# Starting layer 0's output projection with the context tiles inside the last attention block

## The chip, the cores and the metric

The kernel runs on one core of a Trainium2 chip. Five engines work from their own instruction queues and wait for each other through semaphores: TensorE (PE, with its weight loads PEld) for matrix products, VectorE (DVE), ScalarE (ACT), GpSimd (POOL), and SyncE (SP), whose queue issues nearly all DMA transfers here. The metric is the device time of one execution in microseconds (us). The kernel before takes 1860.38 us, the median of three runs between 1852.12 and 1868.84.

## The reference

Two layers over 1024 latent tokens and 256 context tokens of width 1024. Layer 0 is multi-head latent attention with 16 heads, layer 1 differential attention with 8 heads. The core of layer 0 is:

```
q, k, v, gate     = project(h, True)      # 1024 latent tokens, rotary
q_c, k_c, v_c, gate_c = project(h_c, False)   # 256 context tokens
o   = dense_attention(q, concat(k, k_c), concat(v, v_c), scale)
o_c = dense_attention(q_c, k_c, v_c, scale)
x   = layer_norm(ALPHA * x   + gate_x * ((o   * silu(gate))   @ out_w[0]), ln_g, ln_b)
ctx = layer_norm(ALPHA * ctx + gate_c * ((o_c * silu(gate_c)) @ out_w[0]), ln_g, ln_b)
```

The context tokens attend to context keys only, and both streams share the output weights `out_w[0]` and the layer norm.

## The kernel before

Tokens are cut in ten tiles of 128: tiles 0 to 7 are latent, 8 and 9 are context. To keep precision, a float32 matrix is split into a high part and a remainder (`split`, L175 to L177: ACT copies, DVE or POOL subtracts), and a product is the sum of three products (`mm3`, L184 to L187).

**Attention.** For each head h the queries are in three blocks: 0 and 1 are 512 latent tokens each, 2 is the 256 context tokens. `units0` cuts a block into units of two key tiles: five units for blocks 0 and 1, one for block 2. A unit computes scores on PE (L770 to L772), exp and a half-precision copy on ACT (L714, L715), the remainder on POOL (L716), and then 24 products with V on PE (L782 to L785, twelve per key tile). `run_step` writes PE's order by hand: the products with V lag two units behind the scores (`LAG`, `pend`, `retire`), and side work (the maxima of the next block, the projections of the next head) is put between by counts per unit. At a block's end DVE divides by the sum (L793, L794), and after every second head SP stores the pair of heads to `o_d[0]` in DRAM (L798). In the last head the order is blocks 0, 2, 1, with a store for each block.

**Who orders what.** PE's order is the written one inside `run_step`. The orders of ACT, DVE, POOL and SP come from a scheduler that ranks the program's instructions. So work that is written in the last head can be placed earlier, if its data and buffers are ready. `load_outw` (L803 to L808) loads the eight 512 KB slices of `out_w[0]` and splits them on ACT (L807) and DVE (L808); it is written in the last head and needs the space of the projection weights.

**Output of layer 0.** After the last head the attention's buffers and banks are closed. Then `out_tile` runs for tiles 8, 9, 0, ..., 7: load o from `o_d` and the stored silu(gate) g from `sg_d` (L858, L859), multiply on POOL (L860), transpose eight 128x128 blocks on PE (L866), split, multiply by the output weights (24 products for each half of 512 columns, into one bank each), then on DVE gate, residual and statistics (L877 to L879), a power on POOL (L159, L160), and the normalisation (L883). Behind it z is transposed back (L918), scaled and shifted into `hb` (L920 on DVE, L922 on POOL) and split into layer 1's input (L925, L926). For latent tiles the residual of layer 1 is prepared too (L911 to L913). The scaled ln_g and ln_b that this needs are loaded ahead of tile 0 (L905, L906); ln_g takes the buffer `gate01`, which held the context tokens' gate.

```
for t in (8, 9, 0, 1, 2, 3, 4, 5, 6, 7):
    if t == 0:
        for j, (src, tag) in enumerate(((ln_g, "gate01"), (ln_b, "gb1"))):
            gb.append(op0.tile([P, D], F32, tag=tag, bufs=1, name=nm("gb")))
            bcast_row(gb[j], src[0:1, :])
            pool.tensor_scalar(gb[j], gb[j], ALPHA, None, op0=ALU.mult)
    s = 0 if t < 8 else 1
    z = out_tile(t, oH, oL, gate[s], res0, op0)
```

Of the kernel before, what the change touches and what calls it, by code (L numbers as in the profile page):

```python
# [9 lines left out]
F32 = mybir.dt.float32  # L10
# [7 lines left out]
P = 128  # L18
D = 1024
# [34 lines left out]
def hybrid_kernel(  # L54
# [473 lines left out]
    with spool("p0g") as pg:  # L528
# [14 lines left out]
        for _ in side:  # L543
# [23 lines left out]
    cosA = wk.tile([P, SEQ], F32, name="cosA")  # L567
    sinA = wk.tile([P, SEQ], F32, name="sinA")
# [5 lines left out]
    def w0(tag, dt=None):  # L574
        sh, d, b = TAG0[tag]
        return rot(wk, sh, d, tag, b)

    wv = [w0("p32").bitcast(F32R) for _ in range(2)]
    wvs = w0("p32")
    for hh in range(2):  # L580
# [241 lines left out]
            pass  # L822
    man.close()
    ow_ctx = ExitStack()
    for h in range(H0):
        last = h == H0 - 1
        even, quad = (h + 1) % 2 == 0, (h + 1) % 4 == 0
        if last:
            rp.close()
            ow = ow_ctx.enter_context(spool("o0w", side="right"))  # L830
            oH = ow.tile([P, KT, D], F32R, name="oH0")
            oL = ow.tile([P, KT, D], F32R, name="oL0")
            run_step(units0(h, 0) + units0(h, 2), [(max0(h, 2), (1, 0, 1)), (max0(h, 1), (0, 1, 1, 1, 2, 1)),
                                                   (load_outw(oH, oL, lambda: w0("ows")), (1, 2, 2, 2, 1))])
            run_step(units0(h, 1), [])
        else:
            kq = chain(prod_k(h + 1), prod_q(h + 1, 0))
            run_step(units0(h, 0), [(max0(h, 1), (1, 1, 2, 1, 1)), (max0(h, 2), (0, 1, 0, 1)),
                                    (kq, (2, 2, 1 + quad, 0, 0) if even else (2,))])
            qs = chain(prod_q(h + 1, 1), prod_q(h + 1, 2))  # L840
            run_step(units0(h, 1) + units0(h, 2), [(max0(h + 1, 0), (1, 1, 1, 2, 1)),
                                                   (qs, (1, 1 + quad, 0, 1) if even else (2,))])
# [7 lines left out]
    def bcast_row(dst, src):  # L850
        sp.dma_start(dst, src.to_broadcast([P, D]))

    def out_tile(t, oH, oL, gate, res_fn, tp):
# [5 lines left out]
        sp.dma_start(g, sg_d[0][ts, :])  # L859
        pool.tensor_tensor(o, o, g, op=ALU.mult)  # L860
        tH = tp.tile([P, KT, P], F32R, tag="tH", bufs=2, name=nm("tH"))
        tL = tp.tile([P, KT, P], F32R, tag="tL", bufs=2, name=nm("tL"))
        for hh in range(2):
            tb = bank("c")
            for j in range(4):
                pe.transpose(tb[:, j * P:(j + 1) * P], o[:, (hh * 4 + j) * P:(hh * 4 + j + 1) * P], idn)  # L866
            hi = tH[:, hh * 4:hh * 4 + 4, :].rearrange("p a b -> p (a b)")
            split(hi, tL[:, hh * 4:hh * 4 + 4, :].rearrange("p a b -> p (a b)"), tb)
# [3 lines left out]
        for hh in range(2):  # L872
            c = slice(hh * 512, hh * 512 + 512)
            y = bank("ab"[hh])
            for k in range(KT):
                mm3(y, tH[:, k, :], tL[:, k, :], oH[:, k, c], oL[:, k, c], k == 0, k == KT - 1)
            dve.tensor_tensor(z[:, c], y, gate[:, c], op=ALU.mult)  # L877
            dve.scalar_tensor_tensor(z[:, c], res[:, c], rmul, z[:, c], op0=ALU.mult, op1=ALU.add)
            dve.bn_stats(bs[:, hh, :], z[:, c])  # L879
# [3 lines left out]
        dve.tensor_scalar(z, z, mv[:, 0:1], mv[:, 2:3], op0=ALU.subtract, op1=ALU.mult)  # L883
        return z

    with ow_ctx, spool("o0") as op0:
        gate = [op0.tile([P, D], F32, tag=f"gate0{s}", bufs=1, name=f"gate0{s}") for s in range(2)]
        for s in range(2):
            bcast_row(gate[s], gates_d[0, s:s + 1, :])
        gb = []  # L890

        zres = {}

        def res0(t):
            r = op0.tile([P, D], F32, tag="res", bufs=2, name=nm("res"))
            src = xr[t * P:(t + 1) * P, :] if t < 8 else ctxr[(t - 8) * P:(t - 7) * P, :]
            sp.dma_start(r, src)
            zres[t] = r
            return r, ALPHA

        for t in (8, 9, 0, 1, 2, 3, 4, 5, 6, 7):
            if t == 0:
                for j, (src, tag) in enumerate(((ln_g, "gate01"), (ln_b, "gb1"))):
                    gb.append(op0.tile([P, D], F32, tag=tag, bufs=1, name=nm("gb")))
                    bcast_row(gb[j], src[0:1, :])  # L905
                    pool.tensor_scalar(gb[j], gb[j], ALPHA, None, op0=ALU.mult)  # L906
            s = 0 if t < 8 else 1
            z = out_tile(t, oH, oL, gate[s], res0, op0)
            if t < 8:
                zr = zres[t]  # L910
                dve.tensor_tensor(zr, z, gb[0], op=ALU.mult)  # L911
                pool.tensor_tensor(zr, zr, gb[1], op=ALU.add)
                sp.dma_start(zn_d[t * P:(t + 1) * P, :], zr)  # L913
            hb = op0.tile([P, KT, P], F32, tag="hb", bufs=1, name=nm("hb"))
            for hh in range(2):
                tb = bank("d")
                for j in range(4):
                    pe.transpose(tb[:, j * P:(j + 1) * P], z[:, (hh * 4 + j) * P:(hh * 4 + j + 1) * P], idn)  # L918
                ks = slice(hh * 4, hh * 4 + 4)
                dve.tensor_tensor(hb[:, ks, :], tb.rearrange("p (a b) -> p a b", a=4),  # L920
                                  ab1[:, 0, ks, s:s + 1].to_broadcast([P, 4, P]), op=ALU.mult)
                pool.tensor_tensor(hb[:, ks, :], hb[:, ks, :],  # L922
                                   ab1[:, 1, ks, s:s + 1].to_broadcast([P, 4, P]), op=ALU.add)
# [558 lines left out]
```

## Time and profile before

| | us |
|---|---|
| median of three runs | 1860.38 |
| the runs | 1852.12, 1868.84, 1860.38 |
| span of the profiled execution | 1870.0 |
| last product of the attention starts | 804.95 |
| first transposes of output tile 8 / tile 9 / tile 0 | 818.10 / 832.78 / 846.61 |
| last z transposes of the output stage | 973.72 |

The profiled execution is one more execution than the three runs; its span, from the first to the last instruction, is the time that its trace gives. In the rows of a timeline the first number is the start in us from the span's beginning, the second the length. Then come engine, line, operation, output and inputs with their shapes, and in brackets how long the engine stood idle before and what released it. In a group row "x8" is the number of instructions; three numbers with slashes are the shortest, median and longest duration in ns. Names are those of the program without buffer numbers: ps_a to ps_d are PSUM banks, p/ph/pl the exponentials and their two half-precision parts, tH/tL the transposed and split o·g, z the normalised output. PEclk is the share of full speed that TensorE's clock was granted.

### The profile page before, as it was taken

How to read it: one execution, taken by the hardware profiler on the slowest of the kernel's cores; microseconds unless marked ns; L12 is line 12 of the kernel's file. 1: busy time of each engine (PE TensorE's matmuls, PEld its weight loads, DVE VectorE, ACT ScalarE, POOL GpSimd, SP SyncE). 2: the span in 40 equal slices, each digit the busy share in tenths (PEclk: the TensorE clock that was granted, in tenths of full speed). 3: DMA queues.
4: the chain of work that ended last, by engine and by line, in shares of the span. 5: the costliest groups of instructions: out<-in, count | busy, mean ns of one | idle time of the engine just before them, and what ended most of it. 6: DMA issues, size and time to landing. Idle time of an engine off the chain costs nothing. (4 is left out here: it accounts for less than half of the span.)

```text
span 1870.0 us, 36547 instructions
## 1 busy us (share of the span) xinstructions
PE 1696.2 (91%) x14468; PEld 1237.0 (66%) x14468; DVE 1245.6 (67%) x2072; ACT 1077.1 (58%) x2143; POOL 835.2 (45%) x741
## 2 busy tenths in 40 slices
PE   7889998999999998868979999999999999988998
PEld 3888965656666565556756576767666666666776
DVE  7546766565565657526764777787877777878674
ACT  3432047867777787711123667676767676767542
POOL 1443026767767676646662213222222222433654
PEclk9999799999999999979999999999999999999999
DMA  8245630111111113043333222222121212224341
GB/s 307 62 126 182 189 108 18 39 33 36 42 44 32 32 41 100 25 164 123 124 127 106 71 63 66 62 64 58 56 49 44 59 46 61 63 53 139 99 131 68
DMA packets 111225, 154.84 MB, mean 83 GB/s; under 512 B 13415, under 2 KB 84679, under 8 KB 111054
## 3 DMA queue, kind: packets, MB, share of 16 engines
q1 hardware_dynamic: 104238, 146.22, 26.1%
q10 hardware_dynamic: 6816, 6.29, 1.0%
q8 instruction: 114, 1.87, 0.4%
q14 instruction: 57, 0.47, 0.1%
HBM read 98.65 MB, written 27.07 MB: 67 GB/s over the span
## 5 line engine op out<-in xcount | busy, mean ns | idle before, releaser
L716 POOL TENSOR_TENSOR pl<-p,ph 128x1024 f16<-128x1024 f32 (+1 forms) x176 | 362.8, 2066 | 155.9 <-ACT ph L715 129.5
L1167 ACT ACTIVATE p<-ps_b,mx 128x512 f32<-128x512 f32 (+1 forms) x384 | 230.6, 618 | 83.1 <-DVE mx L1163 82.7
L696 DVE TENSOR_REDUCE mx<-ps_a 128x1 f32<-128x1024 f32 x128 | 155.6, 1223 | 138.2 <-PE ps_a L694 138.2
L714 ACT ACTIVATE p<-ps_a,esc 128x1024 f32<-128x1024 f32 (+1 forms) x176 | 189.2, 1075 | 100.4 <-PE ps_a L772 94.5
L715 ACT CAST ph<-p 128x1024 f16<-128x1024 f32 (+1 forms) x176 | 177.1, 1006 | 5.5
L1161 DVE TENSOR_REDUCE mx<-ps_b 128x1 f32<-128x512 f32 x256 | 165.6, 682 | 0.0
L785 PE MATMUL ps_d<-Vh,pl 128*128 128x65 f16 x1344 | 147.5, 195 | 5.2 <-POOL pl L716 5.1
L782 PE MATMUL ps_d<-Vh,ph 128*128 128x65 f16 x1344 | 149.5, 196 | 0.0
L784 PE MATMUL ps_d<-Vl,ph 128*128 128x64 f16 x1344 | 148.3, 193 | 0.0
L185 PE MATMUL ps_b<-h1H,wH 128*128 128x512 f16 (+1 forms) x384 | 133.5, 348 | 14.1 <-DVE pl L182 6.7
L185 PE MATMUL ps_b<-wH,h1H 128*128 128x256 f16 x512 | 139.5, 272 | 4.4 <-ACT p L1167 4.2
L1192 POOL TENSOR_TENSOR sm<-sm,us 128x1 f32<-128x1 f32 x64 | 18.3, 285 | 271.9 <-DVE sm L1171 258.6
L187 PE MATMUL ps_b<-wH,h1L 128*128 128x256 f16 x512 | 139.5, 273 | 0.0
L186 PE MATMUL ps_b<-wL,h1H 128*128 128x256 f16 x512 | 139.5, 272 | 0.0
L1144 PE MATMUL ps_b<-KS,QS 128*128 128x512 f16 (+1 forms) x384 | 126.1, 345 | 12.0 <-DVE pl L182 6.1
L782 PEld LDWEIGHTS <-ph 128*128 128x128 f16 x1344 | 124.2, 98 | 18.4 <-issue 5.5
L187 PE MATMUL ps_b<-h1H,wL 128*128 128x512 f16 (+1 forms) x384 | 133.2, 347 | 0.8 <-DVE wL L182 0.8
L186 PE MATMUL ps_b<-h1L,wH 128*128 128x512 f16 (+1 forms) x384 | 133.4, 347 | 0.0
L784 PEld LDWEIGHTS <-ph 128*128 128x128 f16 x1344 | 124.9, 99 | 12.4 <-issue 0.8
L770 PE MATMUL ps_a<-qH,KH 100*128 100x512 f16 x320 | 123.6, 386 | 9.7 <-ACT p L714 4.3
L1145 PE MATMUL ps_b<-KS,Q 128*128 128x512 f16 (+1 forms) x384 | 129.1, 345 | 0.0
L785 PEld LDWEIGHTS <-pl 128*128 128x128 f16 x1344 | 124.1, 98 | 6.6 <-POOL pl L716 6.5
(370 smaller groups left out, 5161.9 us busy)
## 6 DMA issues: line engine op xcount, KB each, us to landing
ws<-in_dw SPq DMA_DIRECT2D x30, 512.0 KB, 3.8
adw<-in_ada_w SPq DMA_DIRECT2D x24, 512.0 KB, 5.0
g<-sg_d SPq DMA_DIRECT2D x18, 512.0 KB, 3.7
adaw<-in_ada_w SPq DMA_DIRECT2D x16, 512.0 KB, 7.1
sg_d<-gg ACTq DMA_DIRECT2D x40, 128.0 KB, 2.8
o<-o_d SPq DMA_DIRECT2D x10, 512.0 KB, 3.5
o_d<-op SPq DMA_DIRECT2D x7, 640.0 KB, 3.7
xt<-in_xT SPq DMA_DIRECT2D x16, 256.0 KB, 3.6
```

The lines of the kernel that those rows point to most:

```text
L185: pe.matmul(ps, aH, bH, start=start, stop=False, skip_group_check=skip)
L186: pe.matmul(ps, aH, bL, start=False, stop=False, skip_group_check=skip)
L187: pe.matmul(ps, aL, bH, start=False, stop=stop, skip_group_check=skip)
L696: dve.tensor_reduce(mx[:, t, 0:1], ps, axis=AX.X, op=ALU.max)
L714: act.activation(p32[:, :n], st, AF.Exp, scale=esc0)
L715: act.copy(ph[:, :n], p32[:, :n])
L716: pool.tensor_tensor(pl[:, :n], p32[:, :n], ph[:, :n], op=ALU.subtract)
L782: pe.matmul(pv[:, t, :], ph[:, ts], Vh[:, k, h, :], start=(k == kcs[0] and t == 0), stop=False, skip_group_check=True)
L784: pe.matmul(pv[:, t, :V0], ph[:, ts], Vl[:, k, h, :], start=False, stop=False, skip_group_check=True)
L785: pe.matmul(pv[:, t, :], pl[:, ts], Vh[:, k, h, :], start=False, stop=(k == NT - 1), skip_group_check=True)
L1161: dve.tensor_reduce(mx[:, 2 + 2 * m + i:3 + 2 * m + i], b, axis=AX.X, op=ALU.max, negate=True)
L1167: act.activation(p[m][:, c0:c0 + n], b, AF.Exp, bias=nb, accum_out=sm[:, 2 + 3 * m + i:3 + 3 * m + i])
```

## The change

Output tiles 8 and 9 begin inside the last head. `load_outw` is started in head 14 and its steps are spread over heads 14 and 15. The cosine and sine tables move to a rotating tag `cs` of two buffers, so that after the last rotary use these two, `rsw`, `rr` and the two `ows` are free and hold o, g and the transposed parts of both context tiles. During the last block o and g are loaded, DVE multiplies them, and PE takes the transposes and products of both tiles between and behind the last units. The results stay in two pairs of banks (`yctx`) until the output stage, whose `out_tile` is cut in `out_y` (up to the products) and `out_z` (from the gate on). Both context tiles' `out_z` is written ahead of the loop. The banks are set anew after that.

```diff
-            "ows": ([P, D], F32, 2)}
+            "ows": ([P, D], F32, 2), "cs": ([P, SEQ], F32, 2)}
...
+    def turn_out(o, hH_, hL_, tb, hh):
+
+        for j in range(4):
+            pe.transpose(tb[:, j * P:(j + 1) * P], o[:, (hh * 4 + j) * P:(hh * 4 + j + 1) * P], idn)
+        f = lambda x: x[:, hh * 4:hh * 4 + 4, :].rearrange("p a b -> p (a b)")
+        split(f(hH_), f(hL_), tb)
+
+    def mm_out(y, tH, tL, c):
+        for k in range(KT):
+            mm3(y, tH[:, k, :], tL[:, k, :], oH[:, k, c], oL[:, k, c], k == 0, k == KT - 1)
...
-        if last:
+        if h == H0 - 2:
             rp.close()
...
+            lw = load_outw(oH, oL, lambda: w0("ows"))
+        if last:
             run_step(units0(h, 0) + units0(h, 2), [(max0(h, 2), (1, 0, 1)), (max0(h, 1), (0, 1, 1, 1, 2, 1)),
-                                                   (load_outw(oH, oL, lambda: w0("ows")), (1, 2, 2, 2, 1))])
-            run_step(units0(h, 1), [])
+                                                   (lw, (1, 0, 1))])
+            octx = {t: (w0(b_), w0(a_))[::-1] for t, a_, b_ in ((8, "rsw", "rr"), (9, "cs", "cs"))}
+
+            def load_ctx():
+                yield
+                yield
+                for t in (8, 9):
+                    for x, d_ in zip(octx[t], (o_d[0], sg_d[0])):
+                        sp.dma_start(x, d_[t * P:(t + 1) * P, :])
+                    dve.tensor_tensor(*[octx[t][0]] * 2, octx[t][1], op=ALU.mult)
+                yield
+
+            run_step(units0(h, 1), [(load_ctx(), (1, 1, 1))])
+            tv = lambda x: x.bitcast(F32R).rearrange("p (a b) -> p a b", a=KT)
+            tctx = {8: (tv(w0("ows")), tv(w0("ows"))), 9: (tv(w0("rr")), tv(w0("cs")))}
+            with tc.manual_schedule(engines={ENG[c] for c in MAN}):
+                for t in (8, 9):
+                    tb = pair()
+                    for hh in range(2):
+                        turn_out(octx[t][0], *tctx[t], tb[:, hh * 512:hh * 512 + 512], hh)
+                    if t == 8:
+                        retire(0)
+                        retire(1)
+                for t in (8, 9):
+                    yctx[t] = pair()
+                    for hh in range(2):
+                        c = slice(hh * 512, hh * 512 + 512)
+                        mm_out(yctx[t][:, c], *tctx[t], c)
+                        flush()
...
-    flush()
     a0.close()
-    set_banks(a=2, b=2, c=2, d=2)
...
-        for s in range(2):
+        for s in (1, 0):
             bcast_row(gate[s], gates_d[0, s:s + 1, :])
...
+        zctx = {t: out_z([yctx[t][:, :512], yctx[t][:, 512:]], gate[1], res0, t, op0) for t in (8, 9)}
+        set_banks(a=2, b=2, c=2, d=2)
         for t in (8, 9, 0, 1, 2, 3, 4, 5, 6, 7):
...
-            z = out_tile(t, oH, oL, gate[s], res0, op0)
+            z = out_z(out_y(t, op0), gate[0], res0, t, op0) if t < 8 else zctx[t]
```

More of the change, by code (lines that the diff above doesn't have):

```diff
@@ L576, in w0 @@
         return rot(wk, sh, d, tag, b)
+    cosA, sinA = w0("cs"), w0("cs")
     wv = [w0("p32").bitcast(F32R) for _ in range(2)]
@@ L824, in hybrid_kernel, with first @@
     ow_ctx = ExitStack()
+    def first(g, n):
+        for _ in range(n):
+            next(g)
+            yield
[7 more added lines that the diff above has]
+            mm3(y, tH[:, k, :], tL[:, k, :], oH[:, k, c], oL[:, k, c], k == 0, k == KT - 1)
+    yctx = {}
     for h in range(H0):
@@ L836, in hybrid_kernel @@
         else:
             kq = chain(prod_k(h + 1), prod_q(h + 1, 0))
+            low = [[(first(lw, 3), p_)] if h == H0 - 2 else [] for p_ in ((1, 0, 1, 0, 1), (1, 0, 1, 0, 1))]
             run_step(units0(h, 0), [(max0(h, 1), (1, 1, 2, 1, 1)), (max0(h, 2), (0, 1, 0, 1)),
-                                    (kq, (2, 2, 1 + quad, 0, 0) if even else (2,))])
+                                    (kq, (2, 2, 1 + quad, 0, 0) if even else (2,))] + low[0])
             qs = chain(prod_q(h + 1, 1), prod_q(h + 1, 2))
@@ L851, in bcast_row, with out_y @@
         sp.dma_start(dst, src.to_broadcast([P, D]))
-    def out_tile(t, oH, oL, gate, res_fn, tp):
+    def out_y(t, tp):
         ts = slice(t * P, (t + 1) * P)
@@ L863, in out_tile, with out_z @@
         for hh in range(2):
[L864 to L868, printed above, removed]
+            turn_out(o, tH, tL, bank("c"), hh)
+        for hh in range(2):
+            y = bank("ab"[hh])
+            mm_out(y, tH, tL, slice(hh * 512, hh * 512 + 512))
+            yield y
+    def out_z(ys, gate, res_fn, t, tp):
         z = tp.tile([P, D], F32, tag="z", bufs=2, name=nm("z"))
```

10 lines of the change are left out of this document (3 added, 7 removed).

## The prediction

> **What bounds the kernel now.** I read the head of the page first, then the stages around the change.
>
> ```profile
> span 1870.0 us, 36547 instructions
> PE 1696.2 (91%) x14468; PEld 1237.0 (66%) x14468; DVE 1245.6 (67%) x2072; ACT 1077.1 (58%) x2143; POOL 835.2 (45%) x741
> ```
>
> TensorE is busy in 91% of the span; time is won or lost where it stands still. The largest stall near the change is in the waits of PE between 765 and 830 us, and the busy table by stretch shows its place (columns: stretch, length, PE, PEld, DVE, ACT, POOL busy and counts, granted clock, DMA share, GB/s).
>
> ```profile
> PE ps_c L866 <- POOL o L860: 12.9, 1, 12.9
> 803.00:805.00 2.00, 1.19 (x22) 1.20 (x22) 0.00 (x0) 0.00 (x0) 0.75 (x1) 0.59 0.00 0
> 807.00:818.00 11.00, 0.00 (x0) 0.00 (x0) 0.00 (x0) 0.00 (x0) 2.29 (x1) 0.50 0.85 306
> ```
>
> The attention ends at 805.2. Then come a store, six loads that crowd each other and the product o·g on POOL, and only at 818.1 the first transposes of tile 8. The timeline of PE gives the rest of the scale:
>
> ```profile
> 804.95 0.24 PE L785 MATMUL ps_d<-Vh,pl 128*128 128x65 f16 x1
> 818.10 1.97 PE L866 MATMUL ps_c<-idr,o 128*128 128x128 f32 x8 [12.91 <-POOL o L860]
> 823.08 0.63 PE L186 MATMUL ps_a<-oL,tH 128*128 128x512 f32 x1
> 823.51 0.55 PE L187 MATMUL ps_a<-oH,tL 128*128 128x512 f32 x1
> 828.02 0.39 PE L185 MATMUL ps_b<-oH,tH 128*128 128x512 f32 x1
> 828.25 0.39 PE L186 MATMUL ps_b<-oL,tH 128*128 128x512 f32 x1
> 832.78 1.04 PE L866 MATMUL ps_c<-idr,o 128*128 128x128 f32 x8
> 846.61 1.03 PE L866 MATMUL ps_c<-idr,o 128*128 128x128 f32 x8
> 852.05 1.06 PE L918 MATMUL ps_d<-idr,z 128*128 128x128 f32 x8 [0.39 <-DVE z L883]
> ```
>
> A 512-column product starts every 0.23 us at full clock and every 0.43 at half clock, which lasted from 818.1 to about 823.9. A tile's 48 products are 10.9 us; a whole tile costs 13.8 (832.78 to 846.61). The mark for comparison is 846.6: there tile 0's transposes start. Before it lie both context tiles, and of their work only tile 9's z transposes (1.06 and a wait of 0.39 at 852) lie behind.
>
> **Weights from head 14 on: nothing.** In the built order of instructions, ACT and DVE are the same up to the last block, and SP's differs by one early load. The scheduler, not the loop, places these loads:
>
> ```profile
> L807 ACT ACTIVATE oH<-ows,usc x8: 1137/1148/1152, 723.6 to 755.1; 128x1024 fp32r<-128x1024 f32 x8
> 773.01 0.68 ACT L714 ACTIVATE p<-ps_a,esc 128x512 f32<-128x512 f32 x1
> ```
>
> All eight splits already ran before head 14's context block at 773. On PE two pairs of neighbours swap, twelve 65-column products with two or four maximum products: under 0.5 us either way. The load of tile 8's g moves up to head 12 on SP, among loads for a head that starts much later: nothing.
>
> **The front: context tiles inside the last block.** PE takes tile 8's transposes behind the third unit's products (799.9 in this trace), then the fourth unit, tile 9's transposes, half of tile 8's products, the fifth unit, and the other three halves. Everything after the first transpose queues behind its wait for o8·g8.
>
> ```profile
> 793.01 0.29 DVE L794 TENSOR_TENSOR op<-ps_d,rc 128x128 f32<-128x128 f32 x1
> DMA to landing us min/median/max: 1.6/1.9/10.5
> DMA to landing us min/median/max: 3.5/3.5/4.5
> 799.53 4.22 POOL L716 TENSOR_TENSOR pl<-p,ph 128x1024 f16<-128x1024 f32 x2 [0.44 <-ACT ph L715]
> L911 DVE TENSOR_TENSOR res<-z,gb x8: 1224/1224/3292, 866.1 to 973.6; 128x1024 f32<-128x1024 f32 x8
> L808 DVE SCALAR_TENSOR_TENSOR oL<-ows,usc,oH x8: 1271/2072/2983, 724.7 to 756.3; 128x1024 fp32r<-128x1024 f32 x8
> ```
>
> The two landing rows are those of tile o_d (stores and loads together) and of the loads at L858. The context block is divided at 793.3; its store lands after 1.6 to 3.7 us (I take 1.9, the median), so 795.3. SP waits for that, then loads o8, o9, g9: 3.5 to 4.5 each alone, 7.6 in a crowd of six (below); for three I take 4.5, so 800.0. The product moves to DVE. The nearest row alone is L911, 1.22; beside POOL's L716, which runs to 803.75, the nearest is L808, median 2.07, ends 1.27 and 2.98. I take 2.1: PE starts tile 8 at 802.2 (bounds 800 to 806).
>
> Each tile is four transposes, ACT copy, DVE remainder, four transposes, since both halves share one pair of banks: 1.0 + 0.6 + 0.7 + 1.0 at half clock with 0.1 for hand-overs, 3.4. Two tiles and the fourth unit's 24 products at half clock (1.3) end at 810.3. Tile 8's first half starts cold: 5.8 us as from 818.1 on, at 0.43 a start, give 13.5 products, the other 10.5 take 2.4, so 818.5. The fifth unit at full clock is 0.7, and 72 products are 16.4: T, the end of tile 9's products, is 835.6. That is 14 us later for the fifth unit, but its store, the gates and the residuals (four loads) lie under the 16.4 us; uncovered, they would cost the 12.9 again. So far 11.0 us are won against 846.6.
>
> **The back: tile 0 waits for tile 9.** Two queues undo it. On SP, ln_g goes into the buffer of the context gate, so its load waits for DVE's last product with that gate, which waits for T; behind it in the same queue stand ln_b, a residual, and the o and g of tile 0. g of tile 0 also needs the buffer that held tile 9's transposed product. On DVE the four gate products of both tiles stand ahead of tile 8's residual, so both normalisations start at T as well. On POOL, tile 0's o·g stands behind both scalings of ln_g and ln_b and tile 8's two hb additions.
>
> ```profile
> 847.53 0.33 SPq L851 DMA_DIRECT2D gb<-in_ln_g  x1
> 852.12 2.78 POOL L906 TENSOR_SCALAR gb<-gb 128x1024 f32<-128x1024 f32 x1 [1.07 <-DMA gb<-in_ln_g]
> 854.87 2.04 POOL L922 TENSOR_TENSOR hb<-hb,ab 128x512 f32<-128x512 f32 x2
> 880.48 0.55 POOL L160 TENSOR_TENSOR mv<-mv,neghalf 128x1 f32<-128x1 f32 x1
> 880.99 2.35 POOL L860 TENSOR_TENSOR o<-o,g 128x1024 f32<-128x1024 f32 x1
> 881.07 2.83 DVE L883 TENSOR_SCALAR z<-z,mv 128x1024 f32<-128x1024 f32 x1 [0.95 <-POOL mv L160]
> 834.32 0.69 DVE L177 TENSOR_TENSOR tL<-ps_c,tH 128x512 fp32r<-128x512 f32 x1
> 834.92 0.68 DVE L879 BATCH_NORM_STATS2 bs<-z 128x6 f32<-128x512 f32 x1
> 885.08 1.28 DVE L920 TENSOR_TENSOR hb<-ps_d,ab 128x512 f32<-128x512 f32 x2
> 807.89 0.38 SPq L859 DMA_DIRECT2D g<-sg_d  x1
> 815.71 2.34 POOL L860 TENSOR_TENSOR o<-o,g 128x1024 f32<-128x1024 f32 x1 [11.96 <-DMA g<-sg_d]
> ```
>
> DVE starts 512-column operations every 0.6 us. From T, tile 9's two gate products end at 1.35 and ln_g's load is issued. It landed 4.6 us after issue at 847.53; in the crowd at 807.89 a load took 7.6. Five loads now leave within 2 us: I take 5.3, so 6.65. Scaling 2.78 (9.4), the power for tile 8's mv 0.6 (10.0). Tile 8's normalisation now meets ln_b's scaling on POOL; L883 took 2.83 beside a POOL operation that began just ahead and 0.81 without: I take 2.83 (12.85), the nearer row. Then DVE's bn and aggregate of tile 9, 0.9 (13.75), mv on POOL 0.85 (14.6), normalisation 0.81 (15.4), hb of tile 8, 1.3 (16.7), beside which PE does z8's transposes; POOL's second hb half 18.2; o·g 2.35: tile 0's transposes start at T + 20.6 = 856.2 (bounds T + 18.9, with ln_g after 4.6 and L883 at 0.81, and T + 22.9, with ln_g after 7.6). Its own loads, issued by T + 3.7, land by T + 11.3 even in the crowd: hidden under POOL's queue.
>
> **Sum.** 856.2 − 846.6 = +9.6; tile 9's z transposes are done by then: −1.4; tile 0 starts cold after a nearly empty stretch, as tile 8 did: eight transposes 0.95 dearer and 3.8 us at half clock, 1.8: +2.7. Together +10.9 us on the span of 1870.0. That execution's span is 9.6 over the median of the runs, 1860.38; I put the difference on the median: 1871.
>
> **Rivals.** (1) The clock stays full at the front. For it: the waits there are short, 3.0 us ahead of tile 8 and 1.4 within each tile. Against it: in the stretch 803 to 805 the clock had already fallen to 0.59, after PE waits of 1.7 and 1.2 us. Then from 802.2 two tiles cost 2.4 each, the units 0.7 each, 96 products 21.9: T = 830.3, 5.3 us less: 1866. The Trainium skill, "TensorE: Matmul & The Clock Gate", section "Why this matters for your kernels", asks for no idle gap over about 3 us between bursts; by that rule this rival holds, while the trace's 0.59 speaks against it.
>
> (2) Not slower: the remaining tiles lose their collisions.
>
> ```profile
> PE ps_d L918 <- DVE z L883: 10.1, 10, 4.3
> PE ps_a L187 <- DVE tL L177: 5.0, 3, 1.7
> ```
>
> Between 828 and 980 PE waits 5.0 us at three tiles for tL and some 2.2 for z beyond the usual 0.4 and the last 4.3. These come where DVE and POOL meet. Both layer-norm scalings would be gone from that stretch and the phases shift: at most −7.2 from tile 1 on. It decides where T and the back come out short: with rival 1's T and T + 18.9, +10.9 − 5.3 − 1.7 − 7.2 = −3.3: 1857.
>
> (3) Late data: o8·g8 at 806 and T + 22.9 behind: +3.8 and +2.3, 1878.
>
> (4) It does what its words say and nothing is late next: the 12.9 and the cold start (2.7) go, 1845. Against it stands the order on SP, DVE and POOL: tile 0's loads cannot leave before T.
>
> **How the numbers follow.** My forecast 0.45, (1) 0.20, (2) 0.14, (3) 0.16, (4) 0.05. The three runs of before lie from 1852 to 1869, so a median may be off by some 5 us, and about 1% is what a measurement can tell from no change. The range takes in (2) and (3) with that: 1854 to 1884. Slower by over 1% means above 1879, faster below 1841.8: only (3) and the top of the forecast reach the one, only (4) comes near the other.
>
> **What would show it.** In the profile after: DVE's product into rsw ends near 802 and PE's first transposes of `turn_out` follow; PE is busy from some 810 to 836; then about 20 us in which PE has only z8's and z9's transposes, with a wait of tile 0's transposes on POOL's o·g, POOL's gb scaling waiting for ln_g, and L883 near 2.8 beside it; clock near 0.5 in that stretch. The forecast is wrong if tile 0's transposes start before 850 on a like time scale, or if the tiles behind run at another pace than 846 to 974 before.

## The result, and the profile after

The changed kernel takes 1871.13 us, the median of 16 runs from 1863.27 to 1878.9; the kernel before took 1864.2 us in 16 runs beside them (1852.12 to 1868.86). The ratio is 1.0040, with a 95% interval of 1.0027 to 1.0053: 5 to 10 us slower, 6.9 by the medians. The forecast was +10.9 us, to 1871, in a range of 1854 to 1884.

The head of the page of the changed kernel, and the waits of PE between 775 and 860 us (columns: in all, how often, longest):

```profile
span 1862.5 us, 36549 instructions
PE 1691.8 (91%) x14468; PEld 1235.3 (66%) x14468; DVE 1242.1 (67%) x2074; ACT 1077.1 (58%) x2143; POOL 831.5 (45%) x739
```
```profile
PE ps_d L965 <- DVE z L928: 10.7, 2, 10.5
PE ps_c L833 <- POOL o L905: 2.5, 1, 2.5
PE ps_a L833 <- DVE cs L862: 1.7, 1, 1.7
PE ps_a L833 <- DVE ows L177: 1.4, 1, 1.4
```

The wait of 12.9 us for tile 8's o·g is gone. In its place stand small waits inside the last block, and one of 10.5 us for z8, which the kernel before did not have.

**A trap in the page.** This profiled execution is 7.5 us shorter than the one of before (1862.5 against 1870.0), although the median is 6.9 longer. The two profiles already differ ahead of the change: the context block is divided at 781.88 here and at 793.01 there. Over all profiles of this study, whose code before that point does nearly the same work, this division lies anywhere between 777.3 and 793.0 us. So everything below is measured from that division, called C, and both of these kernels were profiled a second time. All times in this table are us behind C:

| kernel | tile 8's transposes | T, end of tile 9's products | tile 0's transposes | tile 1's | last z transposes |
|---|---|---|---|---|---|
| before | 25.1 | – | 53.6 | 67.5 | 180.7 |
| before, second profile | 25.1 | – | 52.9 | 66.8 | 179.8 |
| changed | 7.8 | 40.2 | 58.5 | 72.7 | 181.9 |
| changed, second profile | 9.9 | 40.5 | 58.7 | 73.0 | 185.9 |

Here y8 and y9 are the two context tiles' products with the output weights, z8 and z9 their normalised outputs. T is read from DVE's first product with y9, which starts when PE's last product ends. In the second pair tile 0 starts 5.8 us later and tile 1 starts 6.2 us later than before, and from there to the last z transposes both kernels need 113.0 us. That is the loss that the profiles show.

The back in the changed kernel's first profile: busy time of the engines from T to tile 0 (the clock is third from the end), then the timelines of SP, DVE, POOL and PE.

```profile
822.00:840.40 18.40, 3.95 (x17) 3.13 (x16) 9.90 (x16) 1.04 (x1) 11.70 (x10) 0.64 0.56 199
```
```profile
823.40 0.33 SPq L896 DMA_DIRECT2D gb<-in_ln_g  x1
```
```profile
822.08 1.29 DVE L922 TENSOR_TENSOR z<-ps_a,gate 128x512 f32<-128x512 f32 x2 [9.06 <-PE ps_a L187]
830.83 1.52 DVE L928 TENSOR_SCALAR z<-z,mv 128x1024 f32<-128x1024 f32 x1 [3.20 <-POOL mv L160]
```
```profile
827.46 2.79 POOL L953 TENSOR_SCALAR gb<-gb 128x1024 f32<-128x1024 f32 x1 [0.38 <-DMA gb<-in_ln_g]
830.77 2.78 POOL L953 TENSOR_SCALAR gb<-gb 128x1024 f32<-128x1024 f32 x1
838.01 2.35 POOL L905 TENSOR_TENSOR o<-o,g 128x1024 f32<-128x1024 f32 x1
```
```profile
832.50 1.94 PE L965 MATMUL ps_d<-idr,z 128*128 128x128 f32 x8 [10.46 <-DVE z L928]
835.99 1.97 PE L965 MATMUL ps_d<-idr,z 128*128 128x128 f32 x8 [1.54 <-DVE hb L967]
854.61 1.03 PE L833 MATMUL ps_c<-idr,o 128*128 128x128 f32 x8
```

PE works 4 us in 18.4. The reader finds the forecast's chain link by link: ln_g's load 1.3 us behind T, the scalings on POOL, z8's normalisation just behind the second one, and tile 0's o·g last on POOL.

The kernel before, second profile, and the changed one, second profile (timelines of PE; then DVE of the changed one):

```profile
810.72 1.97 PE L866 MATMUL ps_c<-idr,o 128*128 128x128 f32 x8 [12.92 <-POOL o L860]
838.55 1.03 PE L866 MATMUL ps_c<-idr,o 128*128 128x128 f32 x8
852.42 1.03 PE L866 MATMUL ps_c<-idr,o 128*128 128x128 f32 x8
```
```profile
840.84 1.97 PE L833 MATMUL ps_c<-idr,o 128*128 128x128 f32 x8 [2.45 <-POOL o L905]
855.08 1.03 PE L833 MATMUL ps_c<-idr,o 128*128 128x128 f32 x8
```
```profile
822.66 1.29 DVE L922 TENSOR_TENSOR z<-ps_a,gate 128x512 f32<-128x512 f32 x2 [9.13 <-PE ps_a L187]
```

### The profile page after: what moved, and what is told of

It is laid out like the page before. It is cut to its first block, busy times and chain, and to the rows that moved or that the text cites. A ratio compares the mean times of both kernels' runs of the same rounds, so it can differ in the third digit from the quotient of the medians.

```text
span 1862.5 us, 36549 instructions
## 1 busy us (share of the span) xinstructions
PE 1691.8 (91%) x14468; PEld 1235.3 (66%) x14468; DVE 1242.1 (67%) x2074; ACT 1077.1 (58%) x2143; POOL 831.5 (45%) x739
## 5 line engine op out<-in xcount | busy, mean ns | idle before, releaser
L781 PEld LDWEIGHTS <-ph 128*128 128x128 f16 x1344 | 123.2, 97 | 18.3 <-issue 5.1
L182 DVE SCALAR_TENSOR_TENSOR pl<-ps_b,lcf,ph 128x512 f16<-128x512 f32 (+1 forms) x192 | 117.4, 654 | 16.0 <-ACT ph L181 15.8
```

The costliest lines, as they stand in the source:

```text
L781: pe.matmul(pv[:, t, :], ph[:, ts], Vh[:, k, h, :], start=(k == kcs[0] and t == 0), stop=False, skip_group_check=True)
```

## The experiments

My theory: the change wins at the front what the forecast says, and loses it behind T, where PE has no products queued while DVE and POOL work through both context tiles and then tile 0's o·g. Rivals: that the weights' new place matters; that one load (ln_g) is the whole of the wait; that the loss is the front's own stalls. In the table of results, tile 0 and tile 1 give when their transposes start, by one profile of each kernel; in the kernels with tile 0 ahead of z8, T is where tile 0's transposes start, and for the last two kernels, which have no T, the times are behind C.

| kernel | median us | ratio to before (95%) | tile 0 | tile 1 | last z transposes behind C |
|---|---|---|---|---|---|
| changed, second profile | 1871.1 | 1.0040 (1.0027–1.0053) | T + 18.2 | T + 32.4 | 185.9 |
| weights only | 1863.6 | 1.0005 (0.9985–1.0025) | – | – | 181.8 |
| ln_g's own buffer | 1872.0 | 1.0044 (1.0025–1.0064) | T + 15.9 | T + 31.3 | 183.1 |
| transposes first | 1867.7 | 1.0026 (1.0010–1.0041) | T + 18.3 | T + 32.5 | 185.2 |
| tile 0 first | 1866.2 | 1.0021 (1.0004–1.0037) | T | T + 32.1 | 186.1 |
| tiles 0 and 1 fed | 1882.9 | 1.0118 (1.0095–1.0141) | T | T + 18.6 | 186.3 |
| the same, transposes first | 1880.8 | 1.0097 (1.0074–1.0120) | T | T + 18.9 | 186.6 |
| z8 before T | 1861.8 | 0.9991 (0.9976–1.0005) | T + 5.8 | T + 22.7 | 179.4 |
| y0 ahead | 1869.2 | 1.0024 (1.0008–1.0039) | T + 10.4 | T + 27.9 | 184.5 |
| tile 8's product only | 1857.5 | 0.9966 (0.9949–0.9983) | C + 44.2 | C + 58.1 | 174.0 |
| the same, tile 9's loads first | 1857.8 | 0.9972 (0.9957–0.9987) | C + 45.6 | C + 59.5 | 168.6 |

**1. The weights alone.** The kernel before, with the weights' generator started in head 14:

```diff
-        if last:
+        if h == H0 - 2:
             rp.close()
             ...
+            lw = load_outw(oH, oL, lambda: w0("ows"))
+        if last:
...
-                                                   (load_outw(oH, oL, lambda: w0("ows")), (1, 2, 2, 2, 1))])
+                                                   (lw, (1, 0, 1))])
...
+            low = [[(first(lw, 3), p_)] if h == H0 - 2 else [] for p_ in ((1, 0, 1, 0, 1), (1, 0, 1, 0, 1))]
```

> The kernel before, with only the output weights' splits begun in head 14 and the context tiles left where they were. My theory: the scheduler puts these splits in the same places anyway, so the time is that of before, 1864 us, ratio 1.000 within 0.002. Rival: in the two profiled executions the stretch of head 13 in which the weights are split took 21.7 us before (743.1 to 764.8) and 14.0 after (739.4 to 753.3); if that is the weights' doing and not one execution's clock, this kernel takes 7.7 us less, 1856 us.

Measured: 1863.58 us, ratio 1.0005: no change. The 21.7 us that head 13 took in the first profile of before was one execution's clock: the second profile of before has 14.0 us between the same divisions (743.11 to 757.07), and the clock granted from 743 to 765 us was 0.71 in the first and 1.00 in the second.

**2. Second profiles.** The changed kernel and the kernel before, as they are.

> The changed kernel once more, for a second profile. In the first one DVE's product o8*g8 began 0.08 us ahead of a POOL subtraction and took 1.23 us, ending 7.7 us behind the context block's division; in two of the variants it began 0.6 to 0.7 us behind that subtraction, took 2.5 to 2.6 and ended at 9.7. If the first profile caught a lucky order, it ends near 9.7 here and T, the end of tile 9's products, comes near 40.5 to 42 us behind the division (40.1 in the first); tile 0's transposes start at T + 18 to 19 in any case.

> The kernel before once more, for a second profile. In the first one head 13 took 21.7 us between two divisions (743.1 to 764.8) with the clock at 0.5 for part of it, against 14.0 in the profile of the kernel that has only the weights moved. If that was one execution's clock, it is near 14.0 here; if it belongs to the kernel before, near 21.7. From the context block's division to the last transposes of layer 0 it took 180.7 us there and 181.8 with only the weights moved; I expect 180 to 183.

Measured: as in the first table; one run each, 1866.21 and 1863.05 us. o8·g8 ended 9.7 us behind C, not 7.7. The rows of both profiles, DVE's product and POOL's subtraction at the same place, first profile and then second:

```profile
788.32 1.23 DVE L862 TENSOR_TENSOR rsw<-rsw,rr 128x1024 f32<-128x1024 f32 x1 [6.15 <-DMA rsw<-o_d]
788.40 5.23 POOL L715 TENSOR_TENSOR pl<-p,ph 128x1024 f16<-128x1024 f32 x2 [0.43 <-ACT ph L714]
```
```profile
788.63 5.19 POOL L715 TENSOR_TENSOR pl<-p,ph 128x1024 f16<-128x1024 f32 x2 [0.44 <-ACT ph L714]
789.11 2.73 DVE L862 TENSOR_TENSOR rsw<-rsw,rr 128x1024 f32<-128x1024 f32 x1 [6.71 <-DMA rsw<-o_d]
```

Half a microsecond decides: begun 0.08 us ahead of POOL, the product takes 1.23 us; begun 0.48 behind, 2.73. Such a meeting, in which an operation of DVE or POOL takes longer beside one of the other engine, is called a collision here. It moved T by only 0.3 us, since in the first profile o9·g9 met POOL in its place: 3.13 us, against 1.22 in the second. From C to the last z transposes before took 179.8 us, just under the expected 180 to 183.

**3. ln_g in a buffer of its own.**

```diff
-    with ow_ctx, spool("o0") as op0:
+    with ow_ctx, spool("o0") as op0, spool("o0ln", side="right") as opl:
...
-                    gb.append(op0.tile([P, D], F32, tag=tag, bufs=1, name=nm("gb")))
+                    gb.append((opl if j == 0 else op0).tile([P, D], F32, tag=tag, bufs=1, name=nm("gb")))
```

> The changed kernel with ln_g in a buffer of its own in place of the context gate's; nothing else is moved. Theory (the queues): tile 0 starts T + 18.5 because ln_g's load waits for the last context gate product, and both scalings on POOL and the loads of tile 0 on SP wait behind it. With the buffer the scalings lie before T; tile 0's loads still wait for T (a residual's buffer and the buffer that g shares with tile 9's transposed product), leave by T + 2.5 and land by T + 7, so tile 0's transposes start near T + 10, 8 us earlier: 1863 us. Rival (the order on DVE and POOL, gate products, normalisations and hb additions ahead of tile 0's product, holds it without ln_g): above T + 15, 1868 us or more.

Measured: 1871.95 us, no gain. Tile 0 starts at T + 15.9, not T + 10: the rival stands. POOL's timeline in this kernel (T is 826.1):

```profile
831.19 2.77 POOL L953 TENSOR_SCALAR gb<-gb 128x1024 f32<-128x1024 f32 x1
839.64 2.34 POOL L905 TENSOR_TENSOR o<-o,g 128x1024 f32<-128x1024 f32 x1
```

ln_g's load and scaling now run hundreds of microseconds earlier, and g of tile 0 is issued at 829.52, where loads of g take 3.8 us by the median of the changed kernel's page. Still o·g runs only at 839.64, behind ln_b's scaling, both powers and an hb addition. ln_g's own wait was worth 2.3 of the 18.2 us. The buffer also cost something: from the last z transposes to the end took 901.2 us here against 895.5 to 898.7 in both profiles of before and of the changed kernel. SP's first load of layer 1's `in_dw` weights comes 5.3 us behind the last z transposes here (974.00 against 968.75), and 3.0 ahead of them in both profiles of the changed kernel. That the buffer, held to the last tile, holds up these loads is argued only.

**4. All transposes of a context tile first.** `turn_out` in two parts, both halves' transposes and then both splits:

```diff
-                    for hh in range(2):
-                        turn_out(octx[t][0], *tctx[t], tb[:, hh * 512:hh * 512 + 512], hh)
+                    for part in range(2):
+                        for hh in range(2):
+                            turn_out(octx[t][0], *tctx[t], tb[:, hh * 512:hh * 512 + 512], hh, part)
```

> The changed kernel with all eight transposes of a context tile ahead of the tile's first copy, so that the second four don't wait for the remainder of the first. Theory (the waits of 1.4 us within each context tile are time lost on PE): tile 8's wait turns into a longer wait for tile 9's o9*g9, tile 9's goes, and tile 8's products start 2.5 us earlier: 1868.5 us. Rival (a longer wait in one piece costs the clock what the shorter ones saved): no gain, 1871 us or more.

Measured: 1867.69 us, ratio 1.0026. The median lies where the theory put it, but its interval overlaps the changed kernel's, so a gain in time is not settled. PE's timeline, and a stretch with its clock:

```profile
796.46 1.16 PE L833 MATMUL ps_a<-idr,rsw 128*128 128x128 f32 x8 [2.89 <-DVE rsw L864]
800.24 1.09 PE L833 MATMUL ps_a<-idr,cs 128*128 128x128 f32 x4 [1.31 <-DVE cs L864]
```
```profile
800.00:804.00 4.00, 3.76 (x13) 3.41 (x14) 1.38 (x3) 1.03 (x2) 0.00 (x0) 0.50 0.00 0
```

The waits inside the tiles are gone, but T comes at C + 39.8, only 0.7 us earlier than in the second profile of the changed kernel: the products now begin while the clock is at 0.50, where they began at 1.00 from 798 on there (rows in the next section). The trace stands closer to the rival, and so does the later pair of kernels with tiles 0 and 1 ahead (number 6), which differ in this edit alone: T is C + 40.8 with it and without it.

**5. Tile 0 ahead of both z.** Tile 0's o and g in buffers of their own, its product, transposes and 48 products issued ahead of the context tiles' `out_z`, z8's and z9's transposes behind them. The banks come with it: z8's and z9's transposes take a pair of banks, and `set_banks` moves behind tile 0.

```diff
+        sp.dma_start(o, o_d[0][:P, :])
+        sp.dma_start(g, sg_d[0][:P, :])
+        pool.tensor_tensor(o, o, g, op=ALU.mult)
...
+            mm_out(y0[hh], tH, tL, slice(hh * 512, hh * 512 + 512))
         zctx = {t: out_z([yctx[t][:, :512], yctx[t][:, 512:]], gate[1], res0, t, op0) for t in (8, 9)}
```

> The changed kernel with tile 0's o and g in buffers of their own, its transposes and products ahead of both context tiles' gate products and normalisations, and the transposes of z8 and z9 behind tile 0's products. Theory (what the change loses is the stretch from T to tile 0, in which PE has 4 us of work in 18.5): tile 0 starts within 1.5 us of T, tile 1 at about T + 15 in place of T + 32.7, 18 us earlier: 1853 us, 11 us under the kernel before. Rival (the work of DVE and POOL that is put off, three normalisations and two layer-norm scalings, comes back in the next tiles as collisions): half of it returns, 1862 us or more.

Measured: 1866.22 us, ratio 1.0021. Tile 0 starts at T, as meant, and tile 1 at T + 32.1, where it was. PE's timeline, then a row of DVE:

```profile
829.53 1.03 PE L833 MATMUL ps_a<-idr,o 128*128 128x128 f32 x8
844.74 0.63 PE L985 MATMUL ps_a<-idr,z 128*128 128x128 f32 x4 [2.27 <-DVE z L930]
855.49 1.12 PE L985 MATMUL ps_a<-idr,z 128*128 128x128 f32 x4 [5.90 <-DVE hb L987]
861.65 1.92 PE L833 MATMUL ps_c<-idr,o 128*128 128x128 f32 x8
```
```profile
833.22 2.48 DVE L924 TENSOR_TENSOR z<-ps_a,gate 128x512 f32<-128x512 f32 x4
```

The gap did not go; it moved behind tile 0, where PE meets z8, z9 and z0 in its queue ahead of tile 1. The chain through DVE and POOL had also begun later, behind tile 0's two remainders on DVE: all four gate products run 3.7 us behind T, where y8's ran 10 us ahead of T in the changed kernel (812.24, second profile). And T itself lies at C + 44.0 instead of 40.5. A part of that is o8·g8, which ends at C + 11.6 instead of 9.7: its loads stand behind the load of tile 0's o on SP, and it then meets a subtraction that tile 0's o·g (791.57) has put off on POOL, and takes 3.16 us. The theory's 1853 did not come; the time is in the rival's range, but by this path and not by the collisions that the rival named.

**6. Tiles 0 and 1 both ahead.** o·g of both on POOL before T, and a tile's products between every two pieces of the chain; in a second kernel also the transposes first. The edit changes more than that: all engines work through both context tiles in the written order, ln_g and ln_b have buffers of their own, and both halves of a z are transposed ahead of the additions to `hb`.

```diff
+            early_og(0)
+            z8 = out_z(yc[8], gate[1], res0, 8, op0)
+            early_og(1)
+            y0 = early_y(0, [bank("d"), bank("d")])
+            z9 = out_z(yc[9], gate[1], res0, 9, op0)
...
+            turn_z(8, z8, lambda hh: h_[hh])
+            y1 = early_y(1, halves())
+            h_ = halves()
+            turn_z(9, z9, lambda hh: h_[hh])
```

> The changed kernel with tiles 0 and 1 both put ahead on TensorE: their o and g are loaded into buffers of their own and multiplied on POOL before T (POOL stands idle there for 25 to 40 us), ln_g and ln_b have buffers of their own, and tile 0's 48 products, z8's transposes, tile 1's 48 products, z9's and z0's transposes follow T in this order, so that the chain through DVE and POOL (gate products, normalisations, hb) always has a tile's 12 us of products beside it. Theory (the loss behind T is that chain, wherever TensorE meets it with nothing else queued): tile 1's transposes start near T + 14.5 in place of T + 32.7, and the later tiles keep their pace: 17.5 us less, 1853.5 us, a ratio to before of 0.994 to 0.995. Rival (the chain's work on DVE and POOL comes back as collisions in tiles 2 to 4): 1862 us or more.

> The same with all eight transposes of a context tile ahead of the tile's first copy. Theory: the two gains lie in different stretches and add up, 3.4 us under the kernel with only tiles 0 and 1 put ahead: 1850 us, ratio 0.992 to 0.993. Rival: the front's gain only shifts the phase of later collisions, and the two kernels agree within 1 us.

Measured: 1882.85 and 1880.8 us; both theories were wrong by 30 us. Three rows show two reasons (ACT and PE of the first of the two kernels, then SP of it):

```profile
853.94 1.05 ACT L966 CAST h1H<-hb 128x1024 f16<-128x1024 f32 x1 [18.10 <-POOL hb L963]
```
```profile
855.52 0.80 PE L185 MATMUL ps_a<-oH,tH 128*128 128x512 f32 x1 [6.21 <-ACT tH L176]
```
```profile
980.95 0.43 SPq L1072 DMA_DIRECT2D ws<-in_dw  x1
```

Tile 1's copy on ACT stood behind the copy of tile 8's hb, which waited for POOL, so the chain met PE once more, by another queue. The last z transposes lie at C + 186.3, no earlier than in the changed kernel. And layer 1's first weights were loaded 5.8 us behind the last z transposes (975.15), where the changed kernel's second profile loads them 3.0 ahead (965.05 against 968.03). From the last z transposes to the end took 909.7 us instead of 895.5 to 898.7, which is as much as this kernel loses to the changed one (11.7 us by the medians). The added buffers are the likely cause, not a shown one. What the products put ahead would be worth without them stays open.

**7. z8 before T.** DVE, POOL and SP in the order of the program for both `out_z`:

```diff
-        zctx = {t: out_z([yctx[t][:, :512], yctx[t][:, 512:]], gate[1], res0, t, op0) for t in (8, 9)}
+        with tc.manual_schedule(engines={ENG[c] for c in "DGS"}):
+            zctx = {t: out_z([yctx[t][:, :512], yctx[t][:, 512:]], gate[1], res0, t, op0) for t in (8, 9)}
```

> The changed kernel with DVE, POOL and SP working through tile 8's gate products, residual, statistics and normalisation before tile 9's gate products, in the order of the program, so that z8 is done while TensorE still works on tile 9; the order on SP and POOL changes with it (ln_b's load and scaling and tile 0's o lie ahead of T, tile 0's product ahead of ln_g's scaling). No buffer is added. Theory (behind T, POOL's queue and the order on DVE set the wait, not the data): tile 0's product is done at T + 7, z9 at T + 9, tile 0's products start near T + 10.5 in place of T + 20.5: 9 us less than the changed kernel, 1862 us. Rival (the chain behind T is as long whoever is first): 1869 us or more.

Measured: 1861.8 us, ratio 0.9991 in place of the changed kernel's 1.0040: the 9 us came, and the kernel is as fast as before, within the interval. POOL and PE (T is 824.3):

```profile
827.65 2.35 POOL L905 TENSOR_TENSOR o<-o,g 128x1024 f32<-128x1024 f32 x1 [4.46 <-issue]
```
```profile
833.62 1.94 PE L966 MATMUL ps_d<-idr,z 128*128 128x128 f32 x8 [1.60 <-DVE z L928]
847.02 1.04 PE L833 MATMUL ps_c<-idr,o 128*128 128x128 f32 x8
```

o·g is done at T + 5.7, z9's transposes start at T + 9.3, and tile 0's products behind them at T + 11.3. No buffer and no operation was changed. What held tile 0 was the order in which the engines met the work behind T: y8 had lain ready to be worked on for 9 us before T, and DVE stood in front of y9's gate product instead. Three orders changed together here, so this run does not say which of them is worth how much.

**8. Tile 0's y ahead of the scalings.** Only the order of program text for tile 0:

```diff
             if t == 0:
+                y0 = list(out_y(0, op0))
                 for j, (src, tag) in enumerate(((ln_g, "gate01"), (ln_b, "gb1"))):
```

> The changed kernel with tile 0's loads, product and transposes issued ahead of the loads and scalings of ln_g and ln_b; the context tiles' order on DVE stays. Theory (POOL's queue ahead of tile 0's product costs 11 us of the 18): the product is done at T + 7.5, but mv of tile 9 now stands behind it and ln_g's scaling on POOL, z9 comes at T + 12, and since z9's transposes lie ahead of most of tile 0's products these start near T + 14 in place of T + 20.5: 6 us less, 1865 us. If it is as fast as the one with z8 before T, DVE's order is worth nothing; if it stays at 1870, POOL's order is worth nothing.

Measured: 1869.19 us, ratio 1.0024, 1.9 us under the changed kernel instead of 6. POOL and PE (T is 826.7):

```profile
832.31 2.34 POOL L905 TENSOR_TENSOR o<-o,g 128x1024 f32<-128x1024 f32 x1
```
```profile
841.48 0.74 PE L966 MATMUL ps_d<-idr,z 128*128 128x128 f32 x5 [1.59 <-DVE z L928]
854.61 1.09 PE L833 MATMUL ps_c<-idr,o 128*128 128x128 f32 x8 [1.76 <-POOL o L905]
```

o·g is done at T + 8.0, but z9's transposes come at T + 14.8 and hold most of tile 0's products; tile 1 starts 4.5 us less behind T than in the changed kernel, and at tiles 1 and 2 PE waits for what POOL had put off. Moving tile 0's work forward on POOL and SP alone is worth little: 1.9 us, with intervals that overlap. That DVE's order, which brings z8 and z9 forward, is worth most of the 9 is what is left by subtraction; no run changed DVE's order alone.

**9. Tile 8's product only.** The kernel before, and of the change nothing but tile 8's o·g:

```diff
-            run_step(units0(h, 1), [])
...
+            def load8():
+                yield
+                yield
+                sp.dma_start(o8, o_d[0][8 * P:9 * P, :])
+                sp.dma_start(g8, sg_d[0][8 * P:9 * P, :])
+                dve.tensor_tensor(o8, o8, g8, op=ALU.mult)
+                yield
+
+            run_step(units0(h, 1), [(load8(), (1, 1, 1))])
...
+        o = o8
+        if t != 8:
```

> The kernel before with one thing taken from the change: o and g of tile 8 are loaded inside the last head's last block, right behind the context block's store, and multiplied on DVE there, into two buffers of their own; transposes, products, gates, residuals and all of tile 9 stay where they were. Theory (what the change could win is the wait of 12.9 us for tile 8's o*g; everything else that it moves only puts tile 0 behind tile 9): tile 8's transposes start within 1 us of the attention's end, the clock costs some 2 us at most, and gates, residuals and tile 9's loads land under tile 8's 12.4 us: 12 us less than before, 1851 us, ratio 0.993 to 0.994. Rival (the loads and the gate that tile 8 needs next become the wait): half is lost again, 1857 us. Rival (later tiles' collisions swallow it, as they did with tiles 0 and 1 put ahead): 1862 us or more.

Measured: 1857.48 us, ratio 0.9966: 7.2 us under before, with the next one the fastest of the study. Of the 12 us that the theory expected about half is lost again, as the first rival said. PE's waits between 757 and 815 us, and its timeline (C is 777.32):

```profile
PE ps_d L785 <- POOL pl L716: 5.0, 4, 2.5
PE ps_c L879 <- POOL o L873: 2.4, 1, 2.4
```
```profile
790.01 1.95 PE L879 MATMUL ps_c<-idr,o 128*128 128x128 f32 x8
805.80 1.52 PE L879 MATMUL ps_c<-idr,o 128*128 128x128 f32 x8 [2.42 <-POOL o L873]
```

Tile 8 starts at C + 12.7 instead of 25.1, right behind the attention. Of these 12.4 us some 3 are paid back by tile 0 (C + 44.2 against 52.9 and 53.6, a gain of 8.7 to 9.4): tile 9's o·g now waits for loads in the crowd, with 2.42 us of PE's time. PE's waits for POOL's pl in the attention (four of them from C − 20 on) rise from 3.7 us in the second profile of before to 5.0: DVE's product begins 0.2 us ahead of POOL's last two subtractions, and these take 5.10 us instead of 4.22. Behind tile 1 the last z transposes come after 115.9 us instead of 113.0, so in this profile later collisions, the second rival, took some 3 us as well.

**10. Tile 9's loads first.** In that kernel, tile 9's o and g are loaded ahead of the gates and residuals, and the context tokens' gate ahead of the latent tokens':

```diff
+        sp.dma_start(o9, o_d[0][9 * P:10 * P, :])
+        sp.dma_start(g9, sg_d[0][9 * P:10 * P, :])
+        pool.tensor_tensor(o9, o9, g9, op=ALU.mult)
-        for s in range(2):
+        for s in (1, 0):
             bcast_row(gate[s], gates_d[0, s:s + 1, :])
```

> The kernel with only tile 8's product early, and in it o and g of tile 9 loaded ahead of the gates and residuals, so that the crowd of loads at the attention's end brings first what TensorE asks for first. Theory (tile 9's wait of 2.4 us on its product, which came with loads of some 9 us in a crowd of eight, is the next loss): the wait goes, the gates and residuals still land before the banks of y8 and y9 are wanted, 2.5 us less: 1855 us, ratio 0.995. Rival (the residual now comes later and z8 holds tile 9 or tile 0 instead): no gain, 1857.5 us or more.

Measured: 1857.8 us, ratio 0.9972, as the rival said. PE's waits and DVE's timeline:

```profile
PE ps_d L936 <- DVE z L896: 3.1, 1, 3.1
```
```profile
816.97 0.69 DVE L891 SCALAR_TENSOR_TENSOR z<-res,z 128x512 f32<-128x512 f32 x1 [2.50 <-DMA res<-in_ctxr]
```

The wait for tile 9's product is gone; tile 8's residual now comes last, and PE waits 3.1 us for z8 instead. The profile's early last transposes (C + 168.6) look like one execution with fewer collisions again, since the medians of the two kernels agree.

## Why the prediction was right, point by point

**Weights: nothing.** Right: 1.0005.

**The front.** The forecast for o8·g8's end was C + 9.1 (802.1 on the scale of before); measured 7.7 and 9.7. Tile 9's transposes were to end at C + 17.3, and in the second profile they do (C + 16.1 in the first). PE's and DVE's rows of the second profile, where C is 782.11:

```profile
791.98 0.63 PE L833 MATMUL ps_a<-idr,rsw 128*128 128x128 f32 x4 [2.89 <-DVE rsw L862]
798.74 0.66 PE L833 MATMUL ps_a<-idr,cs 128*128 128x128 f32 x4 [1.40 <-DVE cs L177]
```
```profile
806.01 0.42 DVE L793 TENSOR_TENSOR op<-ps_d,rc 128x256 f32<-128x256 f32 x1
```
 
From there the term "tile 8's first half starts cold: 5.8 us" was too large. The stretches of the second profile, with the clock third from the end:

```profile
790.00:794.00 4.00, 0.63 (x4) 0.42 (x4) 2.57 (x3) 1.18 (x2) 3.83 (x2) 0.97 0.02 8
794.00:798.00 4.00, 3.33 (x32) 2.87 (x32) 1.79 (x3) 1.17 (x2) 0.00 (x0) 0.60 0.00 0
798.00:800.00 2.00, 1.26 (x8) 1.13 (x9) 0.68 (x1) 0.56 (x1) 0.00 (x0) 1.00 0.00 0
```

The clock falls behind the gap that ends at 791.98 and is back at full by 798, before tile 8's first product. That is again some 6 us, but from the first work behind the gap; I had started the 5.8 us at the first product and counted the transposes and the fourth unit at half clock ahead of it as well. The fifth unit is divided at C + 23.9 (806.01) where the forecast has about C + 26.2, and T is C + 40.5 where the forecast had 42.6: 2.1 us too late. The 72 products behind it took what was forecast, 16.6 us against 16.4.

**The back.** The mechanism was right and its size 2.3 us too large: tile 0 starts at T + 18.2, under my lower bound of T + 18.9. ln_g's load was issued as worked out (T + 1.3) but landed 4.1 us after issue instead of 5.3; z8's normalisation, which I put at 2.83, took 1.52. Its moment was no other: both it and the row of 2.83 began 0.06 to 0.08 us behind an operation of POOL. The neighbour was: in that row POOL runs an o·g, here ln_b's scaling. Behind an o·g the normalisation took 2.82 to 2.87 in every profile, behind a scaling 1.52 or 1.53 in the four profiles that have it there; why, no run shows. What the forecast did not see is which link matters. It named SP's queue first; taking ln_g out of the chain gained 2.3 of the 18 us at tile 0 and nothing in time, while changing only the order on DVE, POOL and SP, with z8 made before T, gained 9. The forecast's sentence on DVE, that tile 9's gate products stand ahead of tile 8's residual, names what that run undid; that this carried most of the price is argued, not shown.

**The sum.** Forecast for tile 0 +9.6, measured +5.8 (second pair). The −1.4 for z9's transposes and the cold start belong together: from tile 0 to tile 1 14.2 us, where before took 13.87 with z9's transposes in it. Without these (1.45) that is 12.4, so the cold start cost 1.8, not 2.7. At tile 1 the loss is 6.2 us in place of 10.9, and the medians say 6.9. So both ends of the new path were overestimated by about 2 us each, in the same direction. That 1871 came out all the same is luck: the step was put at 10.9 us and is 6.9, and it was added to a median of three runs, 1860.38, which is 1864.2 in sixteen. Neither sign of a wrong forecast came: in the second profile tile 0 starts at 851.7 on the scale of before, and from there to the last z transposes it takes 127.2 us, against 127.1.

**The rivals.** (1) The clock did not stay full: 0.60 from 794 to 798 in the second profile, behind a wait of 2.89 us. It fell in the first profile too, where no wait of PE in the last block is longer than 1.74 us:

```profile
798.00:800.00 2.00, 2.00 (x7) 1.57 (x6) 0.69 (x1) 0.59 (x1) 0.00 (x0) 0.58 0.00 0
```

The Trainium skill, "TensorE: Matmul & The Clock Gate", section "Why this matters for your kernels", asks for no idle gap over about 3 us between bursts; by that rule the clock need not have fallen in either profile, and the traces do not agree.

The clock recovered so early, though, that T lies almost midway between this rival's C + 37.3 and the forecast. (2) The later tiles' collisions do not vanish: 113.0 us from tile 1 to the last z transposes in both second profiles. The first pair, 113.2 and 109.2, looked as if this rival held; it was one collision less in one execution. (3) o8·g8 was not late, C + 9.7 at most against the C + 13 of this rival (whose sum is 1877, not 1878), (4) and the back was not free.

## What to carry to other kernels

In this kernel, work put ahead in a queue moved the wait behind it. Before work is moved for TensorE, ask what TensorE has queued at the moment when the moved work's results go through the slower engines, and whether those engines could do part of it before. Here the one wait that stood in the profile was worth taking away alone (one product early, 0.9966), and the larger change lost that gain again behind its own end. Compare profiles from a mark next to the change and take a second one: here single profiles differed by up to 16 us ahead of the change, and by 4 us behind it through one collision more or less.

## What the runs showed of the hardware

A DVE product of 128x1024 with two inputs in SBUF took 1.23 us when it began 0.08 us ahead of a POOL subtraction. In eight profiles it began 0.04 to 0.89 us behind the same subtraction, and the later it began the shorter it was, 3.16 down to 2.32 us: it always ended 3.20 or 3.21 us behind the subtraction's start. So it does not share with POOL, it waits POOL out. The Trainium skill, "SBUF — State Buffer", section "🔬 SBUF: two separate sides", calls the port pair that these two engines share an exclusive lock, held for the whole instruction by the one that starts first, for a DVE operation with two SBUF inputs against a GpSimd operation that reads SBUF; for these products the trace agrees. The normalisation of one input does not fit as simply: begun 0.06 us behind a POOL scaling of 2.78 us, it took 1.52 us instead of 0.81 and ended 1.2 us ahead of the scaling.

A stretch in which PE is 16% busy (790 to 794 in the second profile, 0.63 of 4 us) still showed a clock of 0.97; the 0.60 came in the 4 us after it, in which PE was 83% busy, and full speed was back some 6 us behind the end of the gap.
